# Halves of the attention projection weights, made one stage earlier and kept in DRAM

## The chip, the cores and the metric

The kernel is one launch on one core of a Trainium2 chip. The metric is the device time of that launch in microseconds: 3589.42 us before the change, as the median of three timed runs (3587.85, 3589.42 and 3590.59).

## The reference, cut to what matters

A sequence of 1024 tokens with 1024 features passes through two blocks in float32. The first block is an FFN, a token mixer and a second FFN; the second block has two further layers of another kind (called the even and the odd stage), on 16 more tokens. What the change touches is the first FFN and the mixer:

```python
f1 = swiglu(rms_norm(x, g), w_gate, w_up, w_down)       # first FFN, 1024 -> 2816 -> 1024
x = x + 0.5 * rms_norm(f1, g_post)
h = rms_norm(x, mix_pre_g)
fq, fk, fv, fgate, dq, dk, dv = split(h @ w_in)         # 8 "fox" heads, 4 "diff" heads of two halves
fox_o  = causal softmax attention(fq, fk, fv) with decay cumsum(log_sigmoid(fgate + b))
diff_o = rms_norm(attention(q1, k1, v) - lam * attention(q2, k2, v))   # rope on a quarter of q and k
x = x + rms_norm(concat(fox_o, diff_o) @ w_out, mix_post_g)
```

`w_in` is 1024 x 3080 and `w_out` is 1024 x 1024, both float32.

## The kernel before

TensorE multiplies in a faster format that keeps fewer bits (fp32r). To stay exact, each float32 operand `x` is split in two halves: `hi` is `x` rounded to fp32r (a copy on ScalarE, line 224 in the profile), and `lo = x - hi` (a subtraction on VectorE, line 473). A product of two operands is then three matmuls, hi by hi, lo by hi and hi by lo (`mm3`, lines 336 to 338).

The order of all instructions is worked out in Python before the kernel is built. Each piece of work is a generator that yields what it needs: an engine with an estimated duration ("P", "V", "A", "G" for TensorE, VectorE, ScalarE and GpSimd, "D" for the DMA queue that SP issues), a buffer of a pool (`Res`), or an event. A planner (`Sched`) runs these generators with priorities against its own clock and writes down the instructions in the order in which it starts them. On the chip each engine, and SP with its DMA issues, then runs its list strictly in that order and waits wherever an operand isn't there.

The program is a chain of stages: the first FFN (to about 690 us), the mixer (to about 1290), the second FFN, the even and the odd stage.

*First FFN.* Eleven blocks compute the gate and up products (tiles `pst`, weights `w`, `wh`, `wl`), with sums on GpSimd (line 980), and store their result `h` to DRAM (`hD`). The down projection (tiles `pdn`) loads `w_down` and `hD` again (`d`, `dAh`, `dAl`) and splits them (`dh`, `dl`). At its end the residual is added (`acc`, lines 1226 and 1229), the new rows `x` are stored, and the rows are normalised and transposed on TensorE (tile `ptf`, line 577) into the operands `Ah` and `Al` of the next stage. The first 512 tokens are transposed straight from SBUF. The other 512 come back from DRAM as `pt`, once the stores of `x` have landed (`Rows.half1`), are normalised on VectorE (line 626) and transposed in the next stage.

*Weights.* A `Stream` brings weights in units of up to 128x1024: a DMA into one of two raw buffers (`wr`), the copy into `wh` and the subtraction into `wl`, of which there are three pairs. The mixer needs 25 units of `w_in`: 16 of q and k (128x8x128), one for the gate (128x8x8) and 8 of v (128x4x256), in the order of `mixer_weights`. The first three (`NXT`), q and k of the first diff heads and the gate, are loaded and split at the end of the FFN by a Stream called `ahead`. The other 22 are loaded and split in the mixer, between its attention work.

*Halves made ahead.* For `w_out` this is already done otherwise: in the first FFN a low-priority thread, `halves_ahead`, calls `Stream.ahead_of` (lines 507 to 525), which takes both raw buffers, loads 128 rows of `w_out` into one (tile `prer`), copies the high half into the other, subtracts in place, and stores both to a DRAM tile `wo1`. The mixer's output projection (`Attention.out_proj`, `load`) loads these halves. The even stage does the same with the odd stage's `w_out`.

*The turn to the mixer.* The first matmuls of the mixer are `pd` (q of the first diff heads, 48 for each half of the tokens) and `pg` (the gate, 24 for each half). Rope works on `rx` and `ry` with tables `rope` from DRAM; `lt` are the vectors of lambda. `psc` are the scores, `pt` their softmax too, `po` the attention outputs.

Of the kernel before, what the change touches and what calls it, by code (L numbers as in the profile page):

```python
# [18 lines left out]
P = 128  # L19
# [77 lines left out]
def act(n):  # L97
    return 0.07 + 0.92e-3 * n
# [329 lines left out]

class Stream:
# [4 lines left out]
    def __init__(self, c, eng="V", pool=None, nraw=0, nhl=0, shared=True):  # L434
# [4 lines left out]
        self.r_raw, self.r_hl = Res(len(self.raws)), Res(len(self.hls))  # L439
# [39 lines left out]
    def thread(self, items, prio=4):  # L479

        c = self.c
        for key, units in items:
# [3 lines left out]
            for x, srcs in enumerate(units):  # L486
                srcs = srcs if isinstance(srcs, tuple) else (srcs,)
# [19 lines left out]
    def ahead_of(self, w, dst):  # L507

        nc = self.c.nc
        for k in range(KD):  # L510
            yield self.r_raw
            yield self.r_raw
            raw, hi = self.raw("pre"), self.raw("pre", F32R)
# [10 lines left out]
            yield ("D", 1.6)  # L524
            nc.sync.dma_start(dst[1, k], raw)
# [154 lines left out]
def ffn_stage(c, A, first, rows0, wg, wu, wd, gpost, res, rows, nxt, meta=None, cols=None, later=None):  # L680
# [13 lines left out]
    with ExitStack() as ctx:  # L694
# [621 lines left out]
        def halves_ahead():  # L1316
            yield event("prod", 3, 1, "g")
            yield from W.ahead_of(*later)
# [31 lines left out]
class Attention:  # L1350
# [3 lines left out]
    def __init__(self, c, ctx, A, w_in, col0, psb, np_, nth, lo_eng):  # L1354
# [6 lines left out]
        self.W = Stream(c, lo_eng)  # L1361
# [276 lines left out]
    def out_proj(self, oD, w_out, after, ready, evac, last=KD - 1):  # L1638
# [95 lines left out]
def mixer_stage(c, A, rows0, prm, w_in, forget_b, lams, subln, rope, w_out, gpost, res, rows):  # L1734
# [3 lines left out]
    with ExitStack() as ctx:  # L1738
        T = Attention(c, ctx, A, w_in, 0, dict(sc=3, tr=2, po=1, mm=2), 6, 2, "V")
# [155 lines left out]
        items = mixer_weights(w_in)  # L1895
# [254 lines left out]
def odd_stage(c, A, rows0, prm, w_in, w_out, res, final, out):  # L2150
# [3 lines left out]
    with ExitStack() as ctx:  # L2154
        T = Attention(c, ctx, A, w_in, M, dict(sc=3, tr=2, po=1, mm=2), 6, 2, "V")
# [303 lines left out]
def even_stage(c, A, rows0, prm, w_in, lru_wa, lru_wx, dt_bias, a_log, ssd_d, w_out, meta, res, rows, later):  # L2459
# [701 lines left out]
    def weights():  # L3161
        yield from W2.into(w_out, D, WO[0], WO[1], ev_wl, 2, "V")
        yield from W2.ahead_of(*later)
# [15 lines left out]
def kernel(ctx, tc, x, ffn1_pre_g, ffn1_post_g, ffn1_w_gate, ffn1_w_up, ffn1_w_down, mix_pre_g, mix_post_g,  # L3179
# [19 lines left out]
    wo1, wo2 = (c.dr.tile([2, KD, P, D], F32, name=nm) for nm in ("wo1", "wo2"))  # L3199
# [69 lines left out]
```

## Time and profile before

| | |
|---|---|
| timed runs, median (lowest, highest) | 3589.42 us (3587.85, 3590.59) |
| the profiled execution, its own time | 3594.18 us |
| its span from the first to the last instruction | 3592.5 us |
| mean granted clock of TensorE, share of full speed | 0.987 |
| busy share of TensorE, VectorE, ScalarE, GpSimd | 96%, 77%, 47%, 9% |
| chain of waits: TensorE, VectorE, ScalarE | 71%, 19%, 5% |
| bytes read from and written to DRAM | 267.58 MB, 95.13 MB |

The profile comes from one execution, some microseconds longer than the timed runs. A busy share is a mean over stages with different limits, so the stages have to be read one by one: a table of stretches gives each engine's busy time in each. The chain of waits is followed back from the last instruction, at each step to what released it. In the names of the rows, `out<-in` are the tiles written and read; a number in square brackets at the end of a row is the idle time of the engine just before it, with what ended it.

### The profile page before, as it was taken

How to read it: one execution, taken by the hardware profiler on the slowest of the kernel's cores; microseconds unless marked ns; L12 is line 12 of the kernel's file. 1: busy time of each engine (PE TensorE's matmuls, PEld its weight loads, DVE VectorE, ACT ScalarE, POOL GpSimd, SP SyncE). 2: the span in 40 equal slices, each digit the busy share in tenths (PEclk: the TensorE clock that was granted, in tenths of full speed). 3: DMA queues.
4: the chain of work that ended last, by engine and by line, in shares of the span. 5: the costliest groups of instructions: out<-in, count | busy, mean ns of one | idle time of the engine just before them, and what ended most of it. 6: DMA issues, size and time to landing. Idle time of an engine off the chain costs nothing.

```text
span 3592.5 us, 51852 instructions
## 1 busy us (share of the span) xinstructions
PE 3434.7 (96%) x19675; PEld 2929.4 (82%) x19675; DVE 2763.9 (77%) x5074; ACT 1696.3 (47%) x3451; POOL 328.0 (9%) x355
## 2 busy tenths in 40 slices
PE   8899999899999999999999899998999999999998
PEld 6688888778888877888888899988878888888877
DVE  8877689988888769766799779578633788788784
ACT  4333244556666543233345447447422565556551
POOL 0111144000000001111351000000000000000000
PEclk9999999999999999999999999999999999999999
DMA  5452382321211551323562334244473110111133
GB/s 168 146 174 91 103 289 86 123 61 44 67 43 39 178 167 61 122 88 108 178 212 67 111 63 86 61 87 89 139 241 94 57 36 22 39 30 30 34 134 107
DMA packets 305842, 366.07 MB, mean 102 GB/s; under 512 B 18644, under 2 KB 221568, under 8 KB 305592
## 3 DMA queue, kind: packets, MB, share of 16 engines
q1 hardware_dynamic: 299800, 341.71, 30.6%
q10 hardware_dynamic: 5792, 21.04, 1.6%
q8 instruction: 155, 2.54, 0.3%
q14 instruction: 95, 0.78, 0.1%
HBM read 267.58 MB, written 95.13 MB: 101 GB/s over the span
## 4 chain that ended last, share of the span: by engine, by line
PE 71%; DVE 19%; ACT 5%; issue 3%; DMA 2%; SPq 0%; POOL 0%; ACTq 0%; DVEq 0%; POOLq 0%
PE pst L338 7%; PE pst L337 7%; PE pst L336 7%; PE po L1556 3%; PE pe L336 3%; PE pe L338 3%; PE pe L337 3%; DVE kt L2235 3%; PE pdn L337 2%; PE pdn L338 2%; PE pdn L336 2%; PE ptr L1573 2%; DVE dl L1073 2%; PE pwo L3060 2%; PE pwo L3061 2%
## 5 line engine op out<-in xcount | busy, mean ns | idle before, releaser
L336 PE MATMUL pe<-Ah,wh 128*128 128x260 f32 (+1 forms) x1184 | 341.2, 289 | 19.9 <-DVE sz L2561 7.9
L338 PE MATMUL pe<-Ah,wl 128*128 128x260 f32 (+1 forms) x1184 | 337.8, 286 | 0.0
L337 PE MATMUL pe<-Al,wh 128*128 128x260 f32 (+1 forms) x1184 | 337.1, 285 | 0.0
L224 ACT CAST wh<-w 128x512 fp32r<-128x512 f32 x280 | 161.8, 619 | 225.3 <-PE pst L337 137.8
L338 PE MATMUL pst<-Ah,wl 128*128 128x512 f32 x640 | 253.3, 397 | 11.8 <-DVE wl L473 11.8
L916 DVE TENSOR_TENSOR sg<-sg,pst 128x512 f32<-128x512 f32 x280 | 185.9, 680 | 98.4 <-PE pst L338 98.1
L980 POOL TENSOR_TENSOR h<-h 128x512 f32<-128x512 f32 x88 | 137.2, 1560 | 1339.4 <-DVE h L962 1334.3
L337 PE MATMUL pst<-Al,wh 128*128 128x512 f32 x640 | 255.1, 399 | 0.0
L336 PE MATMUL pst<-Ah,wh 128*128 128x512 f32 x640 | 253.9, 397 | 1.2 <-DVE sg L916 1.2
L1524 DVE TENSOR_TENSOR tl<-ptr,th 128x512 fp32r<-128x512 f32 (+2 forms) x344 | 198.6, 591 | 63.9 <-ACT th L224 61.2
L473 DVE TENSOR_TENSOR wl<-w,wh 128x512 fp32r<-128x512 f32 x280 | 211.6, 782 | 44.7 <-ACT wh L224 43.4
L336 PEld LDWEIGHTS pe<-Ah,wh 128*128 128x128 f32 (+1 forms) x1184 | 224.1, 189 | 24.3 <-DVE sz L2561 8.2
L224 ACT CAST th<-ptr 128x512 fp32r<-128x512 f32 (+2 forms) x344 | 171.2, 515 | 147.2 <-PE ptr L1573 137.7
L337 PE MATMUL pdn<-dl,dh 128*128 128x512 f32 x592 | 230.8, 390 | 2.3 <-DVE dl L1073 2.3
L338 PE MATMUL pdn<-dh,dl 128*128 128x512 f32 x592 | 230.3, 389 | 0.0
L336 PE MATMUL pdn<-dh 128*128 128x512 f32 x592 | 229.0, 389 | 0.0
L337 PEld LDWEIGHTS pe<-Al,wh 128*128 128x128 f32 (+1 forms) x1184 | 223.6, 189 | 1.0
L338 PEld LDWEIGHTS pe<-Ah,wl 128*128 128x128 f32 (+1 forms) x1184 | 223.5, 189 | 0.8
L2235 DVE TENSOR_TENSOR_SCAN kt<-kt,onec 128x392 f32<-128x392 f32 (+6 forms) x224 | 202.5, 913 | 25.4 <-ACT kt L224 24.1
L224 ACT CAST wh<-wr 128x1024 fp32r<-128x1024 f32 (+2 forms) x116 | 119.3, 1028 | 167.8 <-PE pwo L3061 75.9
L336 PE MATMUL pst<-T,wh 128*128 128x512 f32 x480 | 187.6, 391 | 2.8 <-ACT T L224 2.8
L338 PE MATMUL pst<-T,wl 128*128 128x512 f32 x480 | 186.7, 390 | 1.1 <-DVE wl L473 1.1
(552 smaller groups left out, 10103.4 us busy)
## 6 DMA issues: line engine op xcount, KB each, us to landing
hD<-h SPq DMA_DIRECT2D x22, 1792.0 KB, 6.2
w<-in_ffn_w_gate_dram SPq DMA_DIRECT2D x20, 1024.0 KB, 5.5
w<-in_ffn_w_up_dram SPq DMA_DIRECT2D x20, 1024.0 KB, 7.8
d<-hD SPq DMA_DIRECT2D x18, 1024.0 KB, 5.5
wr<-in_even_w_in_dram SPq DMA_DIRECT2D x36, 512.0 KB, 4.6
wo<-prer SPq DMA_DIRECT2D x32, 512.0 KB, 3.2
wr<-in_odd_w_in_dram SPq DMA_DIRECT2D x32, 512.0 KB, 4.2
wr<-in_w_in_dram SPq DMA_DIRECT2D x24, 512.0 KB, 3.9
```

The source lines that it names most:

```text
L224: self.last = _o(*a, **k)
L336: nc.tensor.matmul(ps, wh, xh, start=start, stop=False)
L337: nc.tensor.matmul(ps, wh, xl, start=False, stop=False)
L338: nc.tensor.matmul(ps, wl, xh, start=False, stop=stop)
L473: (nc.gpsimd if eng == "G" else nc.vector).tensor_sub(lo, raw, hi.bitcast(F32))
L916: nc.vector.tensor_add(dst, src, ps)
L980: nc.gpsimd.tensor_sub(q[:, o], q[:, a], q[:, b_])
L1073: nc.vector.tensor_sub(lo, v[:, r], hi.bitcast(F32))
L1524: nc.vector.tensor_sub(tl[:rows, :n], ptr[:rows, :n], th[:rows, :n].bitcast(F32))
L1556: nc.tensor.matmul(po[:, 256 - n:256], vs, (th, tl)[which][:rows, o:o + n], start=(x == 0 and y == 0), stop=(x == last and y == len(lhs) - 1))
L1573: nc.tensor.transpose(ptr[:rows, o:o + P], pts[i][:, col:col + rows], c.ident)
L2235: nc.vector.tensor_tensor_scan(rev, rev, c.one.to_broadcast([P, m]), kt[:, k0 + m:k0 + m + 1], op0=ALU.mult, op1=ALU.mult)
```

## The change

The halves of all 25 units of `w_in` are made in the first FFN too, by the same thread and before those of `w_out`, and kept in a DRAM tile `wim`. In the mixer a unit's two halves are loaded straight into `wh` and `wl`, without copy and subtraction. As the mixer then needs no raw buffers, these two serve as a fourth pair of halves (named `wr` in the rows) until the output projection, which takes them back with `give_raw`. The DRAM layout of `wo1` and `wo2` changes from halves outside to units outside. The odd stage keeps its stream as it was. Lines of the kernel after are some 30 to 45 further down: 515 becomes 559, 523 and 525 become 568, 577 becomes 620, 626 becomes 669, and a load of a half is line 525.

```diff
+class Halves:
+    def __init__(self, src, dst):
+        self.src, self.dst, self.shape = src, dst, src.shape
+        self.n = src.shape[1] * src.shape[2]
+
+    @staticmethod
+    def of(c, name, items):
+        n = sum(len(us) for _, us in items)
+        dst = c.dr.tile([n, 2, P, 1024], F32, name=name)
...
 class Stream:
     RAW, HL = 2, 3
...
-        self.r_raw, self.r_hl = Res(len(self.raws)), Res(len(self.hls))
+        if halves:
+            self.hls.append((None, 0))
+        self.r_raw, self.r_hl = Res(0 if halves else len(self.raws)), Res(len(self.hls))
...
     def hl(self, name):
         pool, n = self.hls[self.ihl % len(self.hls)]
         self.ihl += 1
+        if pool is None:
+            return self.raw(name, F32R), self.raw(name, F32R)
...
+    def give_raw(self):
+        if self.hls[-1][0] is None:
+            yield self.r_hl
+            self.hls.pop()
+            for _ in range(len(self.raws)):
+                self.r_raw.release(self.c.sch.time)
...
     def thread(self, items, prio=4):
...
+                if isinstance(srcs, Halves):
+                    m, n = srcs.shape[1], srcs.n
+                    yield self.r_hl
+                    hl = [h[:, :n] for h in self.hl("w")]
+                    for y, h in enumerate(hl):
+                        t = yield ("D", 0.2 + 1.4e-3 * n)
+                        c.nc.sync.dma_start(h.bitcast(F32), srcs.dst[y, :, :n])
+                    if x == len(units) - 1:
+                        self.ev[key].set(t + DMA_IN)
+                    parts.append([h.rearrange("p (k f) -> p k f", k=m) for h in hl])
+                    continue
...
-    def ahead_of(self, w, dst):
+    def ahead_of(self, units):
         nc = self.c.nc
-        for k in range(KD):
+        for u in units:
+            n = u.n
             yield self.r_raw
             yield self.r_raw
...
-            nc.sync.dma_start(raw, w[k * P:k * P + P, :])
+            nc.sync.dma_start(raw.rearrange("p (k f) -> p k f", k=u.shape[1]), u.src)
             yield DMA_IN
-            yield ("A", act(1024))
+            yield ("A", act(n))
             nc.scalar.copy(hi, raw)
-            yield ("V", dve(1024))
+            yield ("V", dve(n))
             nc.vector.tensor_sub(raw.bitcast(F32R), raw, hi.bitcast(F32))
             yield 0.5
-            yield ("D", 1.6)
-            nc.sync.dma_start(dst[0, k], hi.bitcast(F32))
-            yield ("D", 1.6)
-            nc.sync.dma_start(dst[1, k], raw)
+            for x, h in enumerate((hi.bitcast(F32), raw)):
+                yield ("D", 0.2 + 1.4e-3 * n)
+                nc.sync.dma_start(u.dst[x, :, :n], h)
...
         def load():
             yield after
+            yield from W.give_raw()
...
-                    nc.sync.dma_start(WO[x][:, k, :D].bitcast(F32), w_out[x, k])
+                    nc.sync.dma_start(WO[x][:, k, :D].bitcast(F32), w_out[k].dst[x])
...
-    wo1, wo2 = (c.dr.tile([2, KD, P, D], F32, name=nm) for nm in ("wo1", "wo2"))
+    rows_w = lambda w: [("o", [w.rearrange("(k p) f -> p k f", p=P)[:, k:k + 1] for k in range(KD)])]
+    wo1, wo2 = (Halves.of(c, nm, rows_w(w))[1] for nm, w in (("wo1", w_out[0]), ("wo2", odd_w_out_2[0])))
+    mix, mix_u = Halves.of(c, "wim", mixer_weights(w_in[0]))
...
-                   x[0], rows1, mixer_weights(w_in[0])[:NXT], cols=cols,
-                   later=(w_out[0], wo1))
+                   x[0], rows1, mix[:NXT], cols=cols, later=mix_u + wo1)
```

The planner's order changes with it. SP's queue in two blocks of the products, before (`hD` is the store of h, `w` are the weights of the next block):

```order
L982 DMA hD<-h_1662 128x7x512
L736 DMA w<-in_ffn_w_gate_dram 128x8x256
L736 DMA w<-in_ffn_w_up_dram 128x8x256
L982 DMA hD<-h_1950 128x7x512
L736 DMA w<-in_ffn_w_gate_dram 128x8x256
L736 DMA w<-in_ffn_w_up_dram 128x8x256
```

The same place of SP's queue after, one block:

```order
L1025 DMA hD<-h_1090 128x7x512
L559 DMA prer<-in_w_in_dram 128x8x128
L568 DMA wim<-prer 128x1024 x2
L779 DMA w<-in_ffn_w_gate_dram 128x8x256
L779 DMA w<-in_ffn_w_up_dram 128x8x256
L559 DMA prer<-in_w_in_dram 128x8x128
L568 DMA wim<-prer 128x1024 x2
L559 DMA prer<-in_w_in_dram 128x8x128
```

A block now has three loads of `prer`, each with its two stores to `wim`; in the kernel before the eight units of `w_out` all stand ahead of the rows shown, and later blocks have none.

TensorE at the turn to the mixer before, the end of the gate's first half and the first transposes of the second half of the tokens:

```order
L336 MATMUL pg<-Ah,wh 8x512
L337 MATMUL pg<-Al,wh 8x512
L338 MATMUL pg<-Ah,wl 8x512
L577 MATMUL ptf<-ident,pt 128x128 x8
L336 MATMUL pd<-Ah,wh 128x512 x2
L577 MATMUL ptf<-ident,pt 128x128 x4
L337 MATMUL pd<-Al,wh 128x512
L338 MATMUL pd<-Ah,wl 128x512
```

And TensorE at the turn after, from the last matmuls of q's first half on:

```order
L337 MATMUL pd<-Al,wh 128x512
L338 MATMUL pd<-Ah,wl 128x512
L620 MATMUL ptf<-ident,pt 128x128 x12
L336 MATMUL pg<-Ah,wh 8x512
L337 MATMUL pg<-Al,wh 8x512
L620 MATMUL ptf<-ident,pt 128x128 x4
L338 MATMUL pg<-Ah,wl 8x512
L336 MATMUL pg<-Ah,wh 8x512
L337 MATMUL pg<-Al,wh 8x512
L338 MATMUL pg<-Ah,wl 8x512
L620 MATMUL ptf<-ident,pt 128x128 x4
```

The transposes of `pt` moved ahead of the gate's 24 matmuls, which now stand between groups of transposes, and the second half of q moved behind the gate.

SP's queue at the turn before:

```order
L1796 DMA lt<-in_diff_lambda_k_dram 128x64
L1824 DMA rope<-in_rope_dram 128x2x512
L638 DMA pt<-x_98 128x1024 x4
L1824 DMA rope<-in_rope_dram 128x2x512
L496 DMA wr<-in_w_in_dram 128x8x128
```

And SP's queue at the turn after:

```order
L1285 DMA d<-in_x_dram 128x1024 x2
L681 DMA pt<-x_98 128x1024 x4
L1840 DMA lt<-in_diff_lambda_q_dram 128x64
L1840 DMA lt<-in_diff_lambda_k_dram 128x64
L1840 DMA lt<-in_diff_lambda_q_dram 128x64
L1840 DMA lt<-in_diff_lambda_k_dram 128x64
L1868 DMA rope<-in_rope_dram 128x2x512 x2
```

The four loads of `pt`, which wait for the stores of `x`, moved ahead of the loads for lambda and rope.

## Rows read from the trace of the kernel before

**Rows 1.** The page: busy time by engine, and the chain by engine.

```profile
PE 3434.7 (96%) x19675; PEld 2929.4 (82%) x19675; DVE 2763.9 (77%) x5074; ACT 1696.3 (47%) x3451; POOL 328.0 (9%) x355
...
PE 71%; DVE 19%; ACT 5%; issue 3%; DMA 2%; SPq 0%; POOL 0%; ACTq 0%; DVEq 0%; POOLq 0%
```

**Rows 2.** Table of stretches; us, busy of PE, PEld, DVE, ACT, POOL, clock, DMA share.

```profile
150.00:450.00 300.00, 300.00 (x1307) 245.06 (x1306) 209.87 (x316) 93.75 (x162) 51.35 (x32) 1.00 0.39 132
450.00:540.00 90.00, 89.23 (x393) 73.32 (x392) 80.49 (x96) 40.19 (x73) 39.05 (x18) 1.00 0.82 292
550.00:640.00 90.00, 90.00 (x399) 74.55 (x398) 85.57 (x109) 42.22 (x75) 42.52 (x21) 1.00 0.24 76
640.00:690.00 50.00, 46.28 (x206) 37.91 (x204) 49.75 (x88) 28.81 (x59) 0.00 (x0) 0.97 0.32 106
690.00:750.00 60.00, 51.07 (x231) 35.97 (x232) 53.95 (x110) 35.51 (x73) 3.99 (x6) 0.88 0.36 122
750.00:1290.00 540.00, 527.91 (x3234) 450.33 (x3233) 443.54 (x1178) 322.15 (x814) 0.00 (x0) 1.00 0.24 76
```

**Rows 3.** Tile prer, 0 to 300 us: ns min/median/max, first and last start us.

```profile
L515 SPq DMA_DIRECT2D prer<-in_w_out_dram x8: 332/360/1656, 31.4 to 203.0; - x8
L224 ACT CAST prer<-prer x8: 1048/1052/1055, 38.3 to 207.4; 128x1024 fp32r<-128x1024 f32 x8
...
L520 DVE TENSOR_TENSOR prer<-prer x8: 1210/1222/1226, 43.4 to 209.1; 128x1024 fp32r<-128x1024 f32 x8
```

**Rows 4.** Waits of PE, 30 to 230 us: us in total, times, longest.

```profile
PE pst L338 <- DVE wl L473: 11.8, 2, 9.8
```

**Rows 5.** Line 473 in the products, 110 to 480 us.

```profile
L473 DVE TENSOR_TENSOR wl<-w,wh x130: 676/683/1786, 110.3 to 450.9; 128x512 fp32r<-128x512 f32 x130
```

**Rows 6.** Line 473 at the end of the first FFN, 660 to 700 us.

```profile
L473 DVE TENSOR_TENSOR wl<-wr,wh x3: 215/1214/1217, 668.0 to 691.3; 128x1024 fp32r<-128x1024 f32 x2, 128x64 fp32r<-128x64 f32 x1
```

**Rows 7.** Timeline of the turn: start us, us, then idle before and its end.

```profile
707.66 7.73 SPq L638 DMA_DIRECT2D pt<-x  x4
...
715.39 0.92 DVE L626 TENSOR_SCALAR pt<-pt,rs_y 128x1024 f32<-128x1024 f32 x1
...
710.90 0.40 PE L336 MATMUL pg<-Ah,wh 128*8 128x512 f32 x1 [1.05 <-ACT rx L224]
...
716.23 0.39 PE L338 MATMUL pg<-Ah,wl 128*8 128x512 f32 x1
716.47 0.27 PE L577 MATMUL ptf<-ident,pt 128*128 128x128 f32 x1
717.95 0.33 PE L577 MATMUL ptf<-ident,pt 128*128 128x128 f32 x1 [1.22 <-DVE pt L626]
719.53 0.66 PE L577 MATMUL ptf<-ident,pt 128*128 128x128 f32 x4 [1.25 <-DVE pt L626]
721.63 0.69 PE L577 MATMUL ptf<-ident,pt 128*128 128x128 f32 x2 [1.44 <-DVE pt L626]
```

**Rows 8.** Table of stretches of 10 us, around two waits of TensorE.

```profile
90.00:100.00 10.00, 1.53 (x7) 0.94 (x5) 10.00 (x17) 2.47 (x4) 0.00 (x0) 0.83 0.00 0
100.00:110.00 10.00, 6.65 (x15) 4.81 (x16) 10.00 (x18) 2.64 (x5) 0.00 (x0) 0.50 0.00 0
...
720.00:730.00 10.00, 7.99 (x34) 6.24 (x33) 8.26 (x14) 6.10 (x11) 0.00 (x0) 0.66 0.17 55
```

**Rows 9.** Tile wr in the mixer, 700 to 1250 us.

```profile
L224 ACT CAST wh<-wr x22: 1044/1052/1095, 736.9 to 1145.0; 128x1024 fp32r<-128x1024 f32 x22
L473 DVE TENSOR_TENSOR wl<-wr,wh x22: 1194/1216/1226, 740.0 to 1146.1; 128x1024 fp32r<-128x1024 f32 x22
...
DMA to landing us min/median/max: 3.8/3.9/3.9
```

**Rows 10.** Chain of waits in the mixer, 740 to 1290 us: start us, us, what.

```profile
757.58 1.12 DVE wl L473
758.81 0.63 ACT pt L224 x2
...
812.71 1.06 ACT wh L224
...
973.55 1.06 ACT wh L224
...
1098.67 1.13 DVE wl L473
```

More of the change, by code (lines that the diff above doesn't have):

```diff
@@ L426, with place, __init__ @@
 DMA_IN = 2.4
+class Halves:
[6 more added lines that the diff above has]
+        dst = c.dr.tile([n, 2, P, 1024], F32, name=name)
+        units = []
+        def place(u):
+            units.append(Halves(u, dst[len(units)]))
+            return units[-1]
+        return [(key, [place(u) for u in us]) for key, us in items], units
 class Stream:
     RAW, HL = 2, 3
-    def __init__(self, c, eng="V", pool=None, nraw=0, nhl=0, shared=True):
+    def __init__(self, c, eng="V", pool=None, nraw=0, nhl=0, shared=True, halves=False):
         self.c, self.eng = c, eng
@@ L1317, in halves_ahead @@
             yield event("prod", 3, 1, "g")
-            yield from W.ahead_of(*later)
+            yield from W.ahead_of(later)
         def begin():
@@ L1350, with __init__ @@
 class Attention:
-    def __init__(self, c, ctx, A, w_in, col0, psb, np_, nth, lo_eng):
+    def __init__(self, c, ctx, A, w_in, col0, psb, np_, nth, lo_eng, halves):
         self.c, self.A, self.w_in, self.col0 = c, A, w_in, col0
@@ L1360, in __init__ @@
         self.pq, self.pv, self.pp, self.pm = opn("aQ"), opn("aV"), opn("aP"), opn("aM")
-        self.W = Stream(c, lo_eng)
+        self.W = Stream(c, lo_eng, halves=halves)
         self.np, self.nth = np_, nth
@@ L1731, in mixer_weights, with mixer_stage @@
     return items
-def mixer_stage(c, A, rows0, prm, w_in, forget_b, lams, subln, rope, w_out, gpost, res, rows):
+def mixer_stage(c, A, rows0, prm, w_in, items, forget_b, lams, subln, rope, w_out, gpost, res, rows):
     nc, tc, sch = c.nc, c.tc, c.sch
@@ L1738, in mixer_stage @@
     with ExitStack() as ctx:
-        T = Attention(c, ctx, A, w_in, 0, dict(sc=3, tr=2, po=1, mm=2), 6, 2, "V")
+        T = Attention(c, ctx, A, w_in, 0, dict(sc=3, tr=2, po=1, mm=2), 6, 2, "V", True)
         T.identb = prm["identb"]
@@ L1893, in proj @@
             T.event("proj").set(sch.free["P"])
-        items = mixer_weights(w_in)
         for key, _ in items:
@@ L2154, in odd_stage @@
     with ExitStack() as ctx:
-        T = Attention(c, ctx, A, w_in, M, dict(sc=3, tr=2, po=1, mm=2), 6, 2, "V")
+        T = Attention(c, ctx, A, w_in, M, dict(sc=3, tr=2, po=1, mm=2), 6, 2, "V", False)
         T.identb = prm["identb"]
@@ L3162, in weights @@
         yield from W2.into(w_out, D, WO[0], WO[1], ev_wl, 2, "V")
-        yield from W2.ahead_of(*later)
+        yield from W2.ahead_of(later)
     sch.spawn(weights(), 2)
@@ L3204 @@
     A1 = ffn_stage(c, A, True, Start(c, prm["g1"], x[0]), ffn1_w_gate[0], ffn1_w_up[0], ffn1_w_down[0], ffn1_post_g,
-                   x[0], rows1, mixer_weights(w_in[0])[:NXT], cols=cols,
-                   later=(w_out[0], wo1))
+                   x[0], rows1, mix[:NXT], cols=cols, later=mix_u + wo1)
     rows2 = Rows(c, prm["g2"], x2, 0, 0)
-    A2 = mixer_stage(c, A1, rows1, prm, w_in[0], fox_forget_b,
+    A2 = mixer_stage(c, A1, rows1, prm, w_in[0], mix, fox_forget_b,
                      [diff_lambda_q1, diff_lambda_k1, diff_lambda_q2, diff_lambda_k2], diff_subln_g, rope, wo1,
@@ L3230 @@
     A4 = even_stage(c, A3, rows3, prm, even_w_in_2[0], lru_w_a_2[0], lru_w_x_2[0], ssd_dt_bias_2,
-                    ssd_a_log_2, ssd_d_2, even_w_out_2[0], meta_2, x3, rows4, (odd_w_out_2[0], wo2))
+                    ssd_a_log_2, ssd_d_2, even_w_out_2[0], meta_2, x3, rows4, wo2)
     odd_stage(c, A4, rows4, prm, odd_w_in_2[0], wo2, h1,
```

4 lines of the change are left out of this document (2 added, 2 removed).

## The prediction

> **What bounds the kernel now.** I read first the busy shares and the chain of waits: TensorE is busy for 3434.7 of 3592.5 us, and it holds 71% of the chain that ends last, VectorE 19% [rows 1]. So work that moves between VectorE, ScalarE and the DMA queues is worth something only where TensorE stands still, and the whole kernel has 158 us of that. Then I read a table of stretches [rows 2], since the change touches five of them. Between 150 and 450 us (the gate and up products of the first FFN) TensorE is busy for all 300 us and VectorE for 210. At 450 to 540 (end of the products, start of the down projection) the DMA share is 0.82, the highest of the six rows. At 550 to 640 (down projection) TensorE has no gap and VectorE is busy for 85.57 of 90. At 640 to 690 VectorE works 49.75 of 50 us: there it sets the end of the stage. The turn, 690 to 750, leaves TensorE 8.9 us idle at a mean clock of 0.88. In the rest of the mixer, 750 to 1290, TensorE is busy for 527.91 of 540 us, so 12.1 us is the most that any relief of the other engines can give there.
>
> **Products of the first FFN.** A unit of halves takes a load, a cast of 1.05 us on ScalarE, a subtraction of 1.22 us on VectorE and two stores [rows 3]. Before there are 8 such units in this stage, 6 of them loaded between 140 and 203 us; after there are 33, about 25 of them between 150 and 450 us, one in 12 us where before there was one in 10.5, and a load with its two stores stands as before between the h stores and w loads of SP's queue. VectorE gains some 25 x 1.22 = 30 us and ScalarE 26 us in a stretch where they have 90 and 206 us free [rows 2]. The stretch with that density cost TensorE nothing: its only waits on a half before 230 us are 11.8 us on the first weights [rows 4], and from 150 on it has no gap. What SP's queue holds behind a store that waits for its subtraction are the next w loads and the store of h, for which VectorE and GpSimd wait; the cover is the block of matmuls before, with one or two units' work to wait for. I take 0, with 0 to +3.
>
> **End of the products, start of the down projection.** About three units (4.5 MB) now fall beside the first operand loads. At the row's 292 GB/s that is 15 us of transfers, and the queue has 18% of 90 us = 16 us free [rows 2]. I take 0 here and make the rest a rival.
>
> **Down projection.** Five units remain for it. They bring 5 x 1.22 = 6.1 us to VectorE, which has 4.4 us free in 550 to 640 and none afterwards. What doesn't fit runs on into the stretch that VectorE ends: 6.1 - 4.4 = +1.7, from 0 (the units are all spread) to +6.1 (none fits). GpSimd is busy for 42.52 of those 90 us, and a subtraction on VectorE beside it ranges from 676 to 1786 ns round a median of 683 [rows 5]. The Trainium skill ("SBUF — State Buffer", section Who interferes with whom) says that a VectorE instruction with two SBUF inputs contends with a GpSimd instruction that reads SBUF. By that rule half of the five would be stretched by up to 1.1 us, and this term would be some +4.5; the eight units of before never went over 1226 ns, so I keep +1.7.
>
> **Tail of the stage.** The three subtractions for the first q, k and the gate, 1.21 + 1.22 + 0.22 = 2.65 us [rows 6], stand in VectorE's back-to-back stretch before the turn. Now these weights are loaded as halves, and VectorE ends earlier: -2.6 (0 to -2.7).
>
> **The turn.** Here the order changes, not only the load. Before, TensorE finished the first half of q at 709.8 us, then filled the wait for the second half of the tokens with the gate's 24 matmuls, 710.90 to 716.6, and met the first transposes at 716.47. Now the transposes stand in front of the gate on TensorE, the normalisation of pt in front of the rope work on VectorE, and the loads of pt in front of those of lambda and rope on SP. pt comes no sooner: its four loads follow the stores of x, one by one, over 7.73 us, and the first normalised tile is there at 716.3 [rows 7]. So TensorE stands for some 7 us, and the 5.6 us of gate matmuls come later. Between the four tiles they find the waits of 1.22, 1.25 and 1.44 us [rows 7], so of 5.6 us between 1.7 and 5.6 is lost; I take 2.5. The second part is the clock. After a stretch in which TensorE worked 1.53 of 10 us the next 10 us were granted 0.50, that is 1.2 GHz [rows 8]. At half the rate 10 us cost 5; before, the stretch after the shorter waits of this same turn was already granted 0.66, so some of it is paid already: +3 (0 to +5). The Trainium skill ("TensorE: Matmul & The Clock Gate", Part 1) has the throttled state as the default, which activity releases; by that rule the whole +5 would be due, and the trace agrees as far as these rows go. The turn then is +5.5 (+1.7 to +10.6).
>
> **Mixer.** 22 subtractions of 1.216 us and 22 casts of 1.052 us go [rows 9]: 26.8 us of VectorE and 23.1 us of ScalarE. Eight pieces of them lie on the chain, five on VectorE (1.12, 0.53, 1.14, 1.14, 1.13) and three on ScalarE (1.06, 1.05, 1.06), of which the first and the last of each stand in [rows 10]: 8.2 us. Behind most of them something else of the same engine is ready to wait for: 0.1 us after the first piece the chain goes on with a cast of pt [rows 10]. The bounds are 0 and the 12.1 us of TensorE's idle time; with the chain's 8.2 as the nearest row, less about a third for what is late next, I take -5. A unit's two halves of 512 KB each replace one load that landed in 3.9 us [rows 9]; a q or k unit holds TensorE for 48 matmuls, some 11 us, and four pairs of buffers instead of three let three units wait ahead. So I count no wait for them.
>
> **Later stages.** Their order on every engine is as before; 0.
>
> **Sum.** 0 + 0 + 1.7 - 2.6 + 5.5 - 5 = -0.4 us. The profiled execution took 3594.18 us, 1.7 outside its span of 3592.5; it lies 4.8 us above the median of the timed runs, 3589.42. So 3593.8 for an execution like the profiled one, and 3589.0 as a time to compare with the median. What can be told from no change here is 0.2%, 7.2 us: 3582.2 to 3596.6 is "the same".
>
> **Rivals.**
> *Relief wins.* All of the chain's 8.2 us or more comes back in the mixer, and the gate slips into the waits: -2.6 + 1.7 - 8.2 = -9.1, or 3580; with the full 12.1 us, 3576. For it: VectorE works 443.54 of 540 us there, and each piece on the chain is one that TensorE waited behind. Against it: the named waits are short ones on other tiles.
> *The turn loses.* TensorE, VectorE and ScalarE all stop for pt, the gate isn't absorbed, the clock falls, and the down projection is late by what the rule on the shared port gives: 5.6 + 5 + 4.5 - 2.6 - 3 (a weaker mixer) = +9.5, or 3599. It decides from the point where the turn and the down projection together lose more than the 7.6 us that tail and mixer give at my values. For it: the order of all three engines; against it: the waits that the gate can fill.
> *Operands of the down projection late.* The 4.5 MB don't fit into the free 16 us and the first sums wait: half of the 15 us gives +7.5, or 3597. Against it: TensorE was covered by the products to the end of that stretch (89.23 of 90).
> *Halves late in the mixer.* One load time of 3.9 us at each fifth unit is +16, or 3605; the four pairs speak against it. That the change doesn't do what it says I see no way for: the splits are gone from the mixer's order.
>
> **How the numbers follow.** The forecast has 0.43, relief 0.29, the turn 0.18, late operands 0.06, late halves 0.04. The likeliest one's own range is 3583 to 3595. Leaving out the far ends of relief and of the two last cases gives 3577 to 3599. Faster by over 0.2%: 0.30 (relief, with a little of the forecast's lower edge and without its own weak end); the same: 0.44; slower: 0.26 (the turn and the late cases, less their weak ends).
>
> **What would show it.** In the table of stretches 150 to 450 stays at 300 us of TensorE with VectorE near 240. In the turn the gap before the first transposes should be about 7 us and TensorE's clock below 0.88 for 690 to 750; the gate's matmuls should stand between transposes. From 750 on TensorE's idle time should be about 7 us, with no split of weights on the chain and no wait on a half. The prediction is wrong if TensorE waits in the products or at the start of the down projection, if it has a wait for halves in the mixer, or if the mixer's idle time doesn't fall.

## The result, and the profile after

The changed kernel takes 3630.03 us (median of 4 runs, 3627.67 to 3631.88) against 3589.72 us (median of 4) for the kernel before: slower, by a ratio of 1.011 (95% interval 1.0095 to 1.0125). The prediction, 3589.0 us and no change, was wrong by 41 us, and its range ended at 3599. One execution of run e12 below, of 13942.73 us, is left out of its median. The profiled execution has a span of 3629.8 us. Marks in both traces say where it went:

| first start of, us | before | after | later by |
|---|---|---|---|
| the last store of h, end of the products (`hD`) | 481.4 | 516.6 | 35.2 |
| the down projection (`pdn`) | 471.6 | 492.4 | 20.8 |
| the mixer's q (`pd`) | 696.9 | 732.1 | 35.2 |
| the mixer's attention outputs (`po`) | 757.0 | 796.6 | 39.6 |
| end of the span | 3592.5 | 3629.8 | 37.3 |

So the first FFN lost 35 us and the turn 4.4; the mixer, up to its last output matmul, gave 5.0 back. The stages behind it took 2.7 us more (2281.8 us before, 2284.5 after), which is no more than they differ between two runs below that have the later stages of the kernel after (2278.4 in e13, 2284.5 in e14). The same table of stretches as in [rows 2], of the kernel after, with a last row for the mixer from its first attention outputs on:

```profile
150.00:450.00 300.00, 287.61 (x1222) 231.12 (x1222) 209.64 (x302) 97.72 (x161) 56.52 (x28) 0.98 0.61 202
450.00:540.00 90.00, 80.28 (x335) 63.54 (x334) 69.58 (x92) 38.57 (x68) 31.86 (x16) 0.96 0.76 273
550.00:640.00 90.00, 86.87 (x380) 70.66 (x379) 88.56 (x111) 41.59 (x72) 45.98 (x20) 1.00 0.77 263
640.00:690.00 50.00, 50.00 (x222) 41.40 (x221) 47.76 (x65) 26.80 (x47) 16.15 (x6) 1.00 0.07 21
690.00:750.00 60.00, 48.99 (x211) 38.33 (x209) 54.14 (x100) 31.60 (x67) 1.41 (x3) 0.92 0.50 177
797.00:1320.00 523.00, 513.41 (x3158) 438.94 (x3158) 414.47 (x1140) 299.20 (x779) 0.00 (x0) 1.00 0.28 95
```

In the products TensorE has lost the gapless 300 us of [rows 2] and works 287.61. VectorE was forecast to rise to near 240 there (a sum that put 25 units on top of a row that already held 5) and works 209.64, as before: it has 21 of the units' subtractions in it, 16 more, and yet does no more in these 300 us, so it has done less of its other work. It isn't busy but standing. The chain of waits, for one block of the products after, shows on what (start us, us, what):

```profile
301.72 1.63 POOL h L1023
303.85 9.14 DMA prer<-in_w_in_dram
313.15 1.05 ACT prer L224
314.23 1.08 DVE prer L564
315.37 0.68 DVE sg L959
316.57 0.70 DVE wl L505
317.28 7.98 DMA w<-in_ffn_w_up_dram
325.29 0.69 DVE w L828
...
330.78 1.14 DVE prer L564
...
337.23 0.71 DVE h L1005
338.06 3.97 POOL h L1023
...
347.30 8.17 DMA prer<-in_w_in_dram
```

Before, the chain in this stretch was matmuls alone. Now it is a round, a loop through several engines that repeats once in each of the eleven blocks, and it starts again 43.45 us later: GpSimd ends h, the unit's load lands 9.14 us later, ScalarE casts, VectorE subtracts, then makes the FFN's own split that frees a buffer, the w load behind that takes 7.98 us, VectorE works through the block to the next h. SP's queue in the same block:

```profile
303.38 0.37 SPq L1025 DMA_DIRECT2D hD<-h  x1
303.85 0.51 SPq L559 DMA_DIRECT2D prer<-in_w_in_dram  x1
314.22 1.59 SPq L568 DMA_DIRECT2D wim<-prer  x2
316.68 0.38 SPq L779 DMA_DIRECT2D w<-in_ffn_w_gate_dram  x1
317.28 0.54 SPq L779 DMA_DIRECT2D w<-in_ffn_w_up_dram  x1
317.92 1.47 SPq L559 DMA_DIRECT2D prer<-in_w_in_dram  x1
```

From the second on, the stores of h are 41.3 to 43.9 us apart; before, 35.3 to 40.2 us from the fourth on. TensorE's own matmuls of a block take 38.6 us when it has no gap (e13 below). One more thing in the trace of before belongs here: the two blocks in which six of the w_out units ran took 41.3 and 43.9 us between stores of h. TensorE had no gap in them. I read this as a lead, work that lies ready for it and is used up first: the three blocks behind them took 35.3 to 36.3 us, less than the matmuls of a block, and made the 8 us good. The rows that I had read showed its busy time, not the lead.

Where the round holds ScalarE, VectorE and TensorE is in their timelines of this block after (in brackets the idle time just before, and what ended it):

```profile
313.15 1.04 ACT L224 CAST prer<-prer 128x1024 fp32r<-128x1024 f32 x1 [11.74 <-DMA prer<-in_w_in_dram]
314.10 2.17 ACT L224 CAST wh<-w 128x512 fp32r<-128x512 f32 x4
...
311.47 0.69 DVE L1005 TENSOR_TENSOR h<-sg 128x512 f32<-128x512 f32 x1 [7.57 <-DMA hD<-h]
314.23 1.23 DVE L564 TENSOR_TENSOR prer<-prer 128x1024 fp32r<-128x1024 f32 x1 [1.47 <-ACT prer L224]
...
314.76 0.50 PE L336 MATMUL pst<-Ah,wh 128*128 128x512 f32 x1 [1.88 <-ACT wh L224]
316.70 0.50 PE L338 MATMUL pst<-Ah,wl 128*128 128x512 f32 x1 [1.21 <-DVE wl L505]
```

ScalarE stands for 11.74 us before the unit's cast, and the FFN's own casts `wh` are next in its list. VectorE stands for the landing of the store of h (there is one buffer for h) and then for the cast. TensorE's two gaps, 1.88 and 1.21 us, end with the FFN's `wh` and `wl` that had stood behind the unit.

The load stands behind 1.8 MB of h. Two units of the kernel before, the second of them at the same place:

```profile
163.03 0.33 SPq L515 DMA_DIRECT2D prer<-in_w_out_dram  x1
166.68 1.05 ACT L224 CAST prer<-prer 128x1024 fp32r<-128x1024 f32 x1 [1.96 <-DMA prer<-in_w_out_dram]
...
174.05 0.50 SPq L515 DMA_DIRECT2D prer<-in_w_out_dram  x1
182.43 1.05 ACT L224 CAST prer<-prer 128x1024 fp32r<-128x1024 f32 x1 [7.60 <-issue]
```

The first load reached its cast 3.65 us after its issue, the second, issued 0.5 us behind a store of h, after 8.38 us, with ScalarE idle for 7.60 of them. The Trainium skill ("DMA: Bandwidth & Descriptors", section Queues, rings and completion order) says that on each DMA engine a ring's descriptors are consumed in order; the 9.14 us right behind the store, against 3.65 to the cast where no store of h stood just ahead, agree with it.

The turn came as forecast, with the transposes ahead of the gate. TensorE at the turn after, and the clock of the 10 us that follow:

```profile
747.91 0.69 PE L620 MATMUL ptf<-ident,pt 128*128 128x128 f32 x2 [4.41 <-DVE pt L669]
751.98 0.69 PE L620 MATMUL ptf<-ident,pt 128*128 128x128 f32 x2 [3.38 <-DVE pt L669]
...
756.60 1.12 PE L620 MATMUL ptf<-ident,pt 128*128 128x128 f32 x4 [1.35 <-DVE Al L608]
757.36 0.78 PE L336 MATMUL pg<-Ah,wh 128*8 128x512 f32 x1
```
```profile
740.00:750.00 10.00, 4.19 (x18) 2.78 (x16) 6.14 (x13) 4.18 (x11) 1.41 (x3) 0.88 0.86 291
750.00:760.00 10.00, 5.46 (x18) 3.10 (x19) 5.65 (x12) 2.98 (x5) 2.22 (x4) 0.50 0.46 166
```

Where the gate's matmuls filled the wait in [rows 7], TensorE now works 4.19 of 10 us and, in the next 10, 5.46 at a granted clock of 0.50 (1.2 GHz).

### The profile page after: what moved, and what is told of

It reads as the page before. It is cut to its first block, busy times and chain, and to the rows that moved or that the text cites. A ratio compares the mean times of both kernels' runs of the same rounds, so it can differ in the third digit from the quotient of the medians.

```text
span 3629.8 us, 52055 instructions
## 1 busy us (share of the span) xinstructions
PE 3444.6 (95%) x19675; PEld 2928.3 (81%) x19675; DVE 2764.4 (76%) x5074; ACT 1695.8 (47%) x3451; POOL 345.6 (10%) x355
## 4 chain that ended last, share of the span: by engine, by line
PE 59%; DVE 22%; DMA 6%; ACT 6%; issue 5%; POOL 2%; SPq 1%; DVEq 0%; ACTq 0%; POOLq 0%
PE pst L338 3%; PE pst L337 3%; PE pst L336 3%; PE po L1599 3%; PE pe L336 3%; PE pe L338 3%; PE pe L337 3%; DVE kt L2278 3%; DVE dl L1116 2%; PE ptr L1616 2%; PE pwo L3103 2%; PE pwo L3104 2%; DMA w<-in_ffn_w_up_dram 2%; PE pwo L3105 2%; PE pdn L337 2%
## 5 line engine op out<-in xcount | busy, mean ns | idle before, releaser
L1023 POOL TENSOR_TENSOR h<-h 128x512 f32<-128x512 f32 x88 | 150.9, 1715 | 1362.8 <-DVE h L1005 1357.6
L336 PE MATMUL pst<-T,wh 128*128 128x512 f32 x480 | 188.6, 393 | 2.8 <-ACT T L224 2.8
L337 PE MATMUL pst<-T,wh 128*128 128x512 f32 x480 | 188.6, 393 | 0.0
## 6 DMA issues: line engine op xcount, KB each, us to landing
w<-in_ffn_w_gate_dram SPq DMA_DIRECT2D x20, 1024.0 KB, 10.8
```

What stands on the lines that cost most here:

```text
L336: nc.tensor.matmul(ps, wh, xh, start=start, stop=False)
L337: nc.tensor.matmul(ps, wh, xl, start=False, stop=False)
L1023: nc.gpsimd.tensor_sub(q[:, o], q[:, a], q[:, b_])
```

## Experiments

Theory A was that the casts and subtractions of the units hold ScalarE and VectorE, rival B that the transfers and their place in SP's queue do it. In e2 to e5, e7, e11 and e12 the even stage's eight units carry the same edit, which the marks of the first FFN don't see. The mixers of e8, e10 and e13 to e15 have three pairs of halves, as before. The table has the result of every run: units in the first FFN, the median, the ratio to before with its interval, and how much later than before the last store of h, the first `pdn` and the first `pd` start in the profiled execution. A ratio is to runs of the kernel before that were timed with the run (medians 3588.67 to 3590.42 us). The marks are those of one execution, whose time lies up to 6.5 us from the run's median.

| run | units | us | ratio | last h | pdn | pd |
|---|---|---|---|---|---|---|
| after | 33 | 3630.0 | 1.011 (1.0095, 1.0125) | 35.2 | 20.8 | 35.2 |
| e1 mixer only | 9 | 3586.0 | 0.9992 (0.9982, 1.0001) | 0.0 | 0.1 | -3.1 |
| e2 transfers only | 33 | 3589.5 | 1.0002 (0.9992, 1.0011) | -0.7 | -0.3 | -3.9 |
| e3 no stores | 33 | 3605.2 | 1.0046 (1.0031, 1.0061) | 17.6 | 15.4 | 12.8 |
| e4 stores on ScalarE's queue | 33 | 3629.7 | 1.0112 (1.0097, 1.0127) | 42.0 | 31.5 | 39.7 |
| e5 waits only | 33 | 3601.3 | 1.0036 (1.0024, 1.0048) | 7.4 | -2.7 | 2.0 |
| e6 work only | 33 | 3608.3 | 1.0056 (1.0041, 1.0071) | 16.0 | 8.1 | 10.8 |
| e7 late cast | 33 | 3626.5 | 1.0107 (1.0092, 1.0122) | 34.1 | 19.6 | 33.9 |
| e8 every other | 19 | 3596.5 | 1.0021 (1.0011, 1.0031) | 10.5 | 7.6 | 8.6 |
| e10 two a block | 19 | 3609.4 | 1.0051 (1.0037, 1.0065) | 19.6 | 15.8 | 17.7 |
| e11 short subtraction | 33 | 3611.1 | 1.0057 (1.0043, 1.0071) | 18.6 | 4.8 | 14.9 |
| e12 short cast | 33 | 3619.2 | 1.0079 (1.0063, 1.0094) | 25.6 | 14.9 | 26.4 |
| e13 one, behind h | 10 | 3591.7 | 1.0004 (0.9995, 1.0014) | 1.5 | 2.3 | 2.0 |
| e14 one, behind w | 10 | 3591.7 | 1.0004 (0.9995, 1.0013) | 0.1 | 0.3 | -0.1 |
| e15 two, behind w | 19 | 3595.6 | 1.0012 (1.0003, 1.0022) | 7.8 | 2.5 | 5.9 |

**e1.** Only the mixer's side of the change (and all units read one unit's halves):

```diff
-                   x[0], rows1, mix[:NXT], cols=cols, later=mix_u + wo1)
+                   x[0], rows1, mix[:NXT], cols=cols, later=mix_u[:1] + wo1)
```

> The first FFN makes the halves of one w_in unit and of w_out, 9 units instead of 33; the mixer loads halves as in the changed kernel, but all 25 units read the halves of that one unit, so its products are of the wrong weights. It prices the mixer without the extra units. All theories of the first FFN agree: the products and the down projection end as in the kernel before (first pdn near 472 us, first pd near 697). The turn keeps the order of before, so its +4.4 us is gone too. Left is the gain of the mixer: 2 to 9 us, so 3581 to 3588 us. If it comes out above 3595, part of the loss is in the mixer's new loads and not in the first FFN.

3586.0 us; the first FFN's marks are those of before, so all of its loss comes with the extra units. The gain of the mixer, the tail and an undisturbed turn together is 2.9 us, with an interval that just reaches no gain.

**e2.** The unit's cast and subtraction are left out, and the weight is stored twice:

```diff
             yield ("A", act(n))
-            nc.scalar.copy(hi, raw)
             yield ("V", dve(n))
-            nc.vector.tensor_sub(raw.bitcast(F32R), raw, hi.bitcast(F32))
...
-            for x, h in enumerate((hi.bitcast(F32), raw)):
+            for x, h in enumerate((raw, raw)):
```

> The changed kernel with all 33 loads and 66 stores in the first FFN, in nearly the same planned order, but without the casts and subtractions of these units: what is stored as both halves is the weight itself. Theory A (ScalarE and VectorE stand behind casts and subtractions whose load lands late, and the FFN's own splits are queued behind them): most of the 35 us at the first pd goes, 3590 to 3602 us. Theory B (the extra transfers and their place in SP's queue make the loads of w, of h and of the down projection's operands late): it stays, 3615 to 3630 us. In between, 3602 to 3615, both have a share.

3589.5: nothing is lost, so B alone fell. It isn't a clean cut, since without the casts the units found earlier places in SP's queue, and their stores had no cast to wait for: the 25 of w_in are issued from 31.8 to 196.9 us, and all 33 by 253. They were thus denser than in the changed kernel, five or six a block between the second store of h and the fifth, which are 38.6 to 40.6 us apart, and TensorE still had no gap (table of stretches of e2):

```profile
150.00:450.00 300.00, 300.00 (x1307) 245.40 (x1306) 201.12 (x309) 90.01 (x158) 47.61 (x32) 1.00 0.54 188
```

**e3, e4.** The stores left out (but two units' stores, which all loads read), and the stores moved:

```diff
-                nc.sync.dma_start(u.dst[x, :, :n], h)
+                if u in (units[0], units[-1]):
+                    nc.sync.dma_start(u.dst[x, :, :n], h)
```
```diff
-                yield ("D", 0.2 + 1.4e-3 * n)
-                nc.sync.dma_start(u.dst[x, :, :n], h)
+                yield ("A", 0.1)
+                nc.scalar.dma_start(u.dst[x, :, :n], h)
```

> The changed kernel with all loads, casts and subtractions of the 33 units, but with the stores of only two of them; the mixer and the output projection read one unit's halves for all, so their products are of the wrong weights. Theory A: the casts still wait for loads behind the store of h, 3610 to 3630 us. Theory B: 66 stores of 512 KB less in SP's queue and on the DMA queues, so the w loads are on time, 3588 to 3602 us.

> The changed kernel with the stores of the halves issued from ScalarE's DMA queue and not from SP's. SP's queue holds no store that waits for a subtraction any more; the bytes are the same, and the planner fits four units in a block and not three. If the place in SP's queue is the cause (part of theory B), the loss of the products goes: 3590 to 3605 us. If the bytes on the DMA queues are, or ScalarE's waits (theory A, now with the stores' waits on ScalarE too): 3620 to 3650 us.

e3 lies between both. Without the stores five units fit into a block instead of three, and the stores of h are 42.3 to 44.3 us apart as long as there are units (to 400 us), then 32 to 40: so the stores are part of the round, but the smaller loss comes with fewer blocks that have units, not with shorter rounds. e4 gave nothing: SP's queue no longer holds a waiting store, but three or four units a block make rounds of 43.7 to 45.4 us.

**e5, e6.** Theory A in two parts: the wait alone (cast and subtraction on 64 columns), and the work alone (full length, on a resident tile `z`; the code of e6 is shortened):

```diff
-            nc.scalar.copy(hi, raw)
+            nc.scalar.copy(hi[:, :64], raw[:, :64])
...
-            nc.vector.tensor_sub(raw.bitcast(F32R), raw, hi.bitcast(F32))
+            nc.vector.tensor_sub(raw[:, :64].bitcast(F32R), raw[:, :64], hi[:, :64].bitcast(F32))
```
```diff
-            nc.scalar.copy(hi, raw)
+            nc.scalar.copy(a, b)          # a: view of hi, b: z[:, None, :].to_broadcast([P, 2, 512])
...
-            nc.vector.tensor_sub(raw.bitcast(F32R), raw, hi.bitcast(F32))
+            nc.vector.tensor_sub(o, b, a.bitcast(F32))
```

> The changed kernel, in which a unit's cast and subtraction in the first FFN work on 64 of 1024 columns only, so they wait as before but take some 0.25 us each; both stores write the weight itself (so 960 columns of each unit are not split). Theory A1 (the wait: ScalarE, and VectorE behind it, stand still until the unit's load has landed, with the FFN's own splits queued behind): the loss stays, 3612 to 3630 us. Theory A2 (the work: 33 times 1.05 and 1.22 us in front of the FFN's splits): it goes, 3588 to 3600 us.

> The changed kernel, in which a unit's cast and subtraction in the first FFN have their full length but read a resident tile and not the loaded weight, so they don't wait for the load; the stores write the weight and that result, so the low halves are of no use. Theory A1: 3588 to 3600 us. Theory A2: 3612 to 3630 us.

Neither part fell out alone: e5's 3601.3 lies just above the range for the case that only the work costs (to 3600), and e6's 3608.3 between its two ranges. In e5 ScalarE still stood for the units' loads, and yet TensorE had no gap from 150 to 450 us (idle time of the engine before tile `prer` up to 480 us, the changed kernel and then e5; and e5's stretch):

```profile
  DMA prer<-in_w_in_dram: 85.4, 14
...
  DMA prer<-in_w_in_dram: 120.2, 24
```
```profile
150.00:450.00 300.00, 300.00 (x1306) 245.02 (x1305) 206.06 (x326) 87.83 (x176) 49.52 (x32) 1.00 0.65 216
```

(The changed kernel has 34.9 us more there whose end the profile doesn't name.) The blocks of e5, with two to four units each, took 38.3 to 41.4 us, just above TensorE's own. I read this so: a wait costs only as much as the sum of the round is longer than TensorE's block. e6 is not wholly free of waits: its casts stand for the stores of the unit before (76.2 us in 20 waits), and it has three or four units in a block, so it can't price the work by itself.

**e7, e8.** The planner's number for the unit's landing, 2.4 to 9.0; and halves for every other unit only:

```diff
-            yield DMA_IN
+            yield 9.0
             yield ("A", act(n))
```
```diff
+    keep = mix_u[4::2]
+    mix = [(k, [u if u in keep else u.src for u in us]) for k, us in mix]
...
-... later=mix_u + wo1)
+... later=keep + wo1)
```

> The changed kernel with one number of the planner changed: a unit's load in the first FFN is planned to land after 9 us and not 2.4, near what it took on the chip, so its cast stands later in ScalarE's list. Nothing is left out. Theory A1: most of the loss of the products goes, 3592 to 3608 us, with what the down projection still loses. Theory A2: no better than 3620 us.

> The changed kernel with the halves of 11 of the 25 units of w_in (every other one from the fifth on) made in the first FFN, 19 units with those of w_out; the others are loaded and split in the mixer as before. Nothing is left out. The density in a block is the same, three units, but it ends after some seven blocks, and the down projection has none. If the loss adds up block by block from a slack used up (A1 or A2), the products lose about half or less of the 21 us and the down projection nothing: 3588 to 3602 us. If it came from the down projection's units alone: 3586 to 3590 us.

e7 tells nothing of the theories: its trace has the same order on SP, ScalarE, VectorE and GpSimd in the products as the changed kernel's; why the number moved nothing there isn't shown. e8 kept three units a block for five blocks and two in a sixth (40.9 to 43.9 us each) and then came back to 32 to 37: the loss adds up block by block.

**e10, e11, e12.** In e10 each load of a unit is put behind a store of h in SP's list, two units a block (an order alone, no wait). e11 shortens the subtraction of the changed kernel to 64 columns as in e5, e12 the cast.

```diff
+            b = x // per - 1 if per else -1
+            if b >= 0:
+                yield stored(b)
...
+                self.c.tc.add_manual_dep(ld.ins, self.c.hd[b].ins.name, ... NoSync ...)
```

> As e8 (19 units, nothing left out), but each load of a unit is tied in SP's list behind a store of h, so that from the fourth block on two units fall in a block and not three. Theory C (a ring: hD store, unit load, cast, subtraction, the FFN's splits, w load, next unit, h, hD store, through four in-order lists; its round of 43 us with three units is longer than TensorE's block of 36 to 38.6 us): a round with two units is about 43 - 2 to 43 - 5 us, at or under TensorE's block, so stores of h come every 36 to 40 us and the time is 3585 to 3592 us. Theory D (each unit costs a fixed amount, wherever it stands): the same 8 us as e8, 3594 to 3599 us.

> The changed kernel with the full cast, but with a subtraction on 64 of 1024 columns (the low halves are not made in the others): 1 us less on VectorE for each unit, 3 us in a block; the waits stay. Theory C: the round falls from 43.2 to about 40.5 us, and the products lose some 10 of 21 us: 3605 to 3618 us. If VectorE's list alone is the bound: 3592 to 3603 us. If ScalarE's alone: 3622 to 3632 us.

> The changed kernel with a cast of 64 of 1024 columns for each unit and a subtraction of full length that reads that part over and over, and with the weight itself stored twice: 0.8 us less on ScalarE for each unit, 2.4 us in a block; the waits stay. Theory C: the round falls to about 41 us, 3608 to 3620 us. If ScalarE's list alone is the bound: 3592 to 3603 us. If VectorE's alone: 3622 to 3632 us.

e11 and e12 fit a round: 1 us less for each unit on VectorE, or 0.8 us on ScalarE, each shortens it. From the second store of h to the last a block takes 42.6 us in the changed kernel, 41.0 in e11 (three or four units in each) and 41.8 in e12. Neither engine's list alone is the bound, though e12's 3619.2 lies only 3 us from the range that VectorE's alone would give. e10 missed, and with it the round as theory C had priced it: the forecast was 3585 to 3592 us, and two units a block made blocks of 41.8 to 43.6 us, as long as three did. Theory D missed too. SP's queue in a block of e10:

```profile
300.52 0.37 SPq L1032 DMA_DIRECT2D hD<-h  x1
300.98 0.51 SPq L562 DMA_DIRECT2D prer<-in_w_out_dram  x1
311.32 1.58 SPq L574 DMA_DIRECT2D wo<-prer  x2
313.99 0.33 SPq L562 DMA_DIRECT2D prer<-in_w_out_dram  x1
314.42 0.41 SPq L786 DMA_DIRECT2D w<-in_ffn_w_gate_dram  x1
...
344.15 0.37 SPq L1032 DMA_DIRECT2D hD<-h  x1
```

A unit takes both raw buffers, so the second load waits until the first unit is stored. Both units lie one after the other at the start of the round, and the w loads behind them; VectorE stands 9.85 us for the store of h and 3.99 us for the second cast.

**e13, e14, e15.** Number against place: ten units at one a block, behind the store of h or behind the block's w loads; and e10's number behind the w loads.

```diff
+    keep = mix_u[14:16]          # e13, e14; with the 8 units of w_out: 10
...
-            yield from W.ahead_of(later)
+            yield from W.ahead_of(later, 1, lambda b: event("hD", b))           # e13
+            yield from W.ahead_of(later, 1, lambda b: event("raw", b + 2, "u"))  # e14; e15 with 2 and mix_u[4::2]
```

> 10 units in the first FFN (2 of w_in, 8 of w_out), nothing left out, each load tied in SP's list behind the store of h of its block, so one unit a block, right behind a store of 1.8 MB. Theory E (the place: a unit's load right behind the store of h lands 8 to 10 us later, its cast and subtraction hold ScalarE and VectorE for that time, and the FFN's splits and the w loads come late): stores of h every 39 to 42 us in the blocks with a unit, and 3594 to 3604 us. Theory C or D (each unit adds about 1.5 to 2 us to a round, which a block with one unit still covers): stores of h every 36 to 39 us and 3586 to 3592 us.

> The same 10 units, nothing left out, one a block, but each load tied in SP's list behind the block's w loads and not behind the store of h. Theory E: the wait falls where VectorE has work ahead of it and the w loads are already on their way, so stores of h every 36 to 39 us and 3585 to 3592 us, 6 to 12 us under the run with the units behind the store of h. Theory C or D: the same as that run within 2 us.

> The 19 units of e8 and e10, nothing left out, up to two a block, tied behind the w loads. Theory E: the later blocks, where no load stands right behind a store of h, take 36 to 39 us, and the time is 3587 to 3598 us, well under the 3609 of e10. Theory D: 3605 to 3612 us.

Theory E, that the place alone decides, fell: e13 and e14 are equal, with stores of h every 38.6 us (in e14 from the fourth on), TensorE's own block. One unit a block fits at either place. With two the place counts. e15 has three units in four blocks (41.3 to 43.5 us) and then two in two blocks, which take 40.4 and 38.7 us; TensorE has no gap in the second. e10's five blocks with two take 41.8 to 43.6 us. SP's queue in the second of e15:

```profile
342.19 0.37 SPq L1032 DMA_DIRECT2D hD<-h  x1
351.01 0.38 SPq L786 DMA_DIRECT2D w<-in_ffn_w_gate_dram  x1
...
352.11 1.41 SPq L562 DMA_DIRECT2D prer<-in_w_out_dram  x1
...
366.41 0.38 SPq L562 DMA_DIRECT2D prer<-in_w_out_dram  x1
...
380.87 0.37 SPq L1032 DMA_DIRECT2D hD<-h  x1
```

So I take the sum of the round against TensorE's 38.6 us as what decides: one unit fits, two behind the w loads nearly or just fit (two blocks of e15 are all that show it), two ahead of them or three do not. The sum itself was never forecast rightly for two units; it was read afterwards. Not tested is a second pair of raw buffers, or a second buffer for h, which would cut the round at another place. No run here beats the kernel before clear of noise. e1 sets the limit, about 3 us with the units for nothing, and the round has room for about one unit a block.

## Why the prediction was wrong

**Products: the step that failed.** "The cover is the block of matmuls before ... I take 0, with 0 to +3." They cost 20.8 us by the first `pdn` and 35.2 by the last store of h, when the down projection has begun. I had reckoned the units as busy time against free time (30 of 90 us on VectorE), and took [rows 3, 4] as proof that this density costs nothing. Both miss what an in-order list does: a unit is a serial piece, load, cast, subtraction, stores, through the only pair of raw buffers, and whatever it waits for holds the FFN's splits queued behind. The round that this makes, through SP, ScalarE, VectorE and GpSimd, is 43 us, where TensorE's block is 38.6, and TensorE then waits for the FFN's `wh` and `wl` (12.8 us in twelve waits from 150 to 490 us). The prediction did name what stands behind a waiting store on SP, but gave it no price. What would have priced it is the distance between stores of h in the two blocks of before that had units, 41.3 and 43.9 us, and the load that took 8.38 us to its cast in the second of them. After, the first gap in the products behind 150 us is in 250 to 300 us, three to four blocks on.

**Start of the down projection: 0 was wrong too.** TensorE in the first stretch after the first `pdn`, before and then after:

```profile
471.60:530.00 58.40, 58.40 (x259) 48.36 (x258) 54.78 (x71) 31.46 (x57) 22.67 (x12) 1.00 0.95 341
492.40:560.00 67.60, 58.35 (x243) 46.16 (x242) 59.95 (x75) 31.87 (x59) 28.96 (x14) 0.95 0.86 316
```

It has lost 9.25 us there, where it lost nothing before. The longest gap, with what stood ahead of it on GpSimd and ScalarE:

```profile
497.83 5.86 POOL L1073 TENSOR_TENSOR d<-d 128x1024 f32<-128x1024 f32 x3 [22.59 <-DMA d<-in_ffn_w_down_dram]
500.28 1.04 ACT L224 CAST prer<-prer 128x1024 fp32r<-128x1024 f32 x1 [4.65 <-DMA prer<-in_w_out_dram]
502.42 0.79 PE L336 MATMUL pdn<-dh 128*128 128x512 f32 x1 [4.37 <-ACT dh L224]
```

So the rival of late operands, priced at +7.5 and given 0.06, happened in part: GpSimd stood for a load of `w_down`. But the cast `dh` that TensorE waited for is also next in ScalarE's list behind a unit's cast, which stood for its load: the same list as in the products. How the gap divides between the two isn't shown. e2 doesn't exclude the transfers here, as its own are over before the down projection begins.

**Down projection: +1.7 - 2.6 against +14.4.** `pdn` starts 20.8 us late and `pd` 35.2. Of these 14.4 us, 9.3 are more idle time of TensorE, nearly all in the stretch above; the other 5.1 are busy time of the same number of matmuls, some of them at a granted clock of 0.66 (500 to 510 us). The three kernels that load five units after the first `pdn` (the changed one, e7, e12) lose 11.5 to 14.4 us between `pdn` and `pd`; the nine whose last unit is loaded over 20 us before it lose between -3.6 and +3.4, and the three in between (e4, e5, e11) 4.7 to 10.1. So most of this goes with the units there, and it comes as waits, where I had counted VectorE's 6.1 us of work against its free time. In the fifteen kernels of the table `pd` is later by what the last store of h is later, within 5.4 us, so a late end of the products may have a share; no run takes those units alone.

**Tail and mixer: the sum right in the profiles, in part by luck.** `pd` starts 3.1 us earlier in e1, where -2.6 was the forecast for the tail. The mixer's part from the first `po` to its last output matmul (1310.7 us before, 1345.3 after) took 5.0 us less in the profiles; -5 was the forecast. No split of weights and no wait on a half is left there. But TensorE's idle time, which was to fall from 12.1 to 7 us, is 9.6 of 523 us, against 11.6 of the same 523 us behind the first `po` before: 2 us of the 5.0 are the relief that I had meant, the other 3 are less busy time of TensorE, which I had not forecast. In timed runs e1's 2.9 us, with the tail in it, is less than the 7.6 that I had counted for both. In e1's profile `po` starts only 0.7 us earlier, so the turn gives back most of the tail; the rest of the difference stays open. (In every profile of a kernel that loads all 25 units' halves, the mixer's part took 4.9 to 7.5 us less than before.)

**Turn: right.** +5.5 forecast, 4.4 measured from `pd` to `po`, with the order, the waits (9.0 us on pt) and the clock as described (mean 0.89 from 735 to 797 us, 0.93 in the same part before). Other runs bear it out: the eight kernels with the new order of TensorE at the turn (the changed one, e2, e3, e5 to e7, e11, e12) take 1.9 to 5.8 us more from `pd` to `po`, the seven with the order of before (e1, e4, e8, e10, e13 to e15) between -0.7 and +2.4. These are single executions, so the size stays open by some 2 us. The Trainium skill ("TensorE: Matmul & The Clock Gate", Part 1) has the throttled state as the default, which activity releases; the 0.50 in the 10 us after those in which TensorE worked 4.19 us agrees.

**The rivals.** The right side was the slower one, at 0.26, but none of its mechanisms was that of the products. A rival "in-order lists behind the units" belonged there: ScalarE's idle time before `prer`, 13.3 us for loads and 12.5 more, stood in the answer from which [rows 3] come, and I had left it as idle time of an engine that isn't the bottleneck.

## What to carry to other kernels

Free time of an in-order engine is not room for work that waits: write the round (store, load, cast, subtraction, next load) as a chain and compare its sum with the block of the bound engine. A gapless busy share over a few blocks proves nothing while a lead is being spent; look at the distance between events that occur once a block. Work made ahead must be spread so that the round stays under the block, here one unit a block.

## What the runs showed that was not expected

A load of 512 KB that reached its cast 3.65 us after its issue elsewhere took 9.14 and 8.17 us to land behind a 1.8 MB store in the same queue (the two in the chain of the block after). And some 50 MB of loads and stores in the first 264 us of e2, at a DMA share of 0.54 from 150 to 450 us, left TensorE's 300 us whole: in e2 the bytes were free, and what cost time in the changed kernel came with the instructions that touched them.
